# Weights in pieces of 1 MB with runs of 8192 bytes per partition, and two load buffers of 8 KB in place of three or four of 4 KB

## The chip, the cores and the metric

The kernel runs on one core of a Trainium2 chip. The metric is the device time in microseconds (us) of one execution, as the median of several runs. TensorE is PE in the profile (PEld its weight loads), VectorE is DVE, ScalarE is ACT, GpSimd is POOL, and SyncE is SP, which issues nearly all plain DMAs. In the trace, L263 means line 263 of the kernel before.

## The reference, cut to what matters

```python
def _layer(x, mem_k, mem_v, C0, n0, m0, ...):
    xn = _rmsnorm(x, g_mix)
    p = xn @ w_in + b_in                       # 1024 x 9224
    q, k, v, ig, fg, og, su, sv, xq, gates = jnp.split(p, _split_points(), axis=-1)
    ...                                        # h_a: mLSTM, h_b: spatial gating, h_c: cross-attention
    merged = g[:, :, 0] * h_a + g[:, :, 1] * h_b + g[:, :, 2] * h_c
    x = x + merged @ w_out                     # 1024 x 1024
    x = x + _peer(_rmsnorm(x, g_ffn), w_pq, k_sub1, k_sub2, u_exp, v_exp)

def _peer(xn, w_pq, k_sub1, k_sub2, u_exp, v_exp):
    q = xn @ w_pq                              # 1024 x 2048
    v1, i1 = top_k(q1 @ k_sub1.T, 16)          # 8 heads, 128 keys on each side
    v2, i2 = top_k(q2 @ k_sub2.T, 16)
    sc, pos = top_k(v1[:, None] + v2[None, :], 16)
    e, g = expert indices, softmax(sc)         # 128 of 16384 experts for each token
    a = gelu(einsum('tkd,td->tk', u_exp[e], xn))
    return einsum('tk,tkd->td', g * a, v_exp[e])
```

The layer runs for 1024 prompt tokens and 64 sample tokens with the same weights. `w_mk` and `w_mv` (1024 x 1024 each) make the memory's keys and values for the prompt. All data is float32.

## The kernel before

The tokens are nine tiles: eight of 128 rows (0 to 7) and "s" with 64. They go through the layer in three blocks, [0, 1], [2, 3, 4, s] and [5, 6, 7]. **The dense weights** are read once per block. A list `pieces` holds them in the order of use: 16 pieces for the memory, then 96 for each block (`w_in`, `w_out`, `w_pq`), then the experts. A piece is 512 KB: 128 partitions by two rows of 512 columns for `w_in` and its like (runs of 2048 bytes), by four rows of 256 columns for `u_exp_t` (runs of 1024 bytes), by two rows of 512 columns for `v_exp` (2048).

`w_load` (L253) issues one piece on SP into `wraw`, which has three buffers of 4 KB per partition; in the last stage every fourth piece goes into a fourth buffer, `wrawx`. `w_split` (L267) takes 512 columns at a time, a split, and makes two fp32r halves of it: ACT casts `wh` (L277) and DVE subtracts for `wl` (L280; 32 of them run on POOL). `wh` and `wl` have four buffers each. When the last split of a piece is done, the next `w_load` is issued. `w_get` (L287) hands a split to the matmuls: `proj_t` (L311 to L313), `proj_T` (L328 to L330), and in the last stage `hidden` (L1119 to L1121) and `dense` (L1268 to L1270), three matmuls for each product.

**The experts** are computed in two ways. For tiles 0, 1, s, 6 and 7 rows of `u_exp` and `v_exp` are gathered by POOL (L1025, 128 rows of 4096 bytes in one indirect DMA, 1152 of them) into three buffers `gu` and four `gv`, and DVE multiplies and adds them up (L1038 for u, L1046 for v). This stream (`experts`) runs beside the blocks and beside the last stage. At the 576th gather it halts until the signal "weights". For tiles 2 to 5, all 16384 experts are computed densely in the last stage: `dense` builds one-hot weights by matmul (L1210), stores them (L1221), loads them again in pieces of 1 MB with runs of 8192 bytes (L1098), and runs the two big products.

Between a block's projections and its gathers stand `retrieve` and `choose_tile`: the top 16 of every head by DVE's max, max_index and match_replace (`top16`, L797 to L803), with a work buffer `tk` (four buffers), the places `pos`, and the softmax `gg` (`ggd`). `end_u` (L954) makes a tile's gather weights, `w2` (two buffers).

Generators for these streams are merged in program order by `Flow`, with an estimated cost at each yield. Then the tile framework's scheduler sets each engine's order, and places waits where a buffer is still in use. Each engine runs its list strictly in order; SP's list holds the weight loads, the small loads and the stores together.

Of the kernel before, what the change touches and what calls it, by code (L numbers as in the profile page):

```python
# [18 lines left out]
D = 1024  # L19
# [46 lines left out]
def tile_stream_step(ctx: ExitStack, tc: tile.TileContext, a: dict, out: dict):  # L66
# [26 lines left out]
    RAW, HL = 3, 4  # L93
# [53 lines left out]
    G.dma_start(wg_raw, a["w_in"][:, O_IG:O_IG + 8].rearrange("(k p) c -> p k c", p=128))  # L147
# [96 lines left out]
    def want(src, c0):  # L244
        for kp in range(4):
            pieces.append(src[kp * 256:(kp + 1) * 256, c0:c0 + 512].rearrange("(k p) c -> p k c", p=128))
# [6 lines left out]
    def w_load():  # L253
        i = W["load"]
        if i >= len(pieces):
            return
        src = pieces[i]

        if now["dp"] is None or i % (RAW + 1):
            t = wp.tile([128, D], F32, name="wraw", bufs=RAW)  # L260
        else:
            t = now["dp"].tile([128, D], F32, name="wrawx")
        SP.dma_start(t.rearrange("p (k c) -> p k c", k=src.shape[1]), src)  # L263
        raw_t[i] = t
        W["load"] += 1

    def w_split():  # L267
        i = W["split"]
        if i >= 2 * len(pieces):
            return  # L270
        p, kk = divmod(i, 2)
        while W["load"] <= p:
            w_load()
        t = raw_t[p][:, kk * 512:(kk + 1) * 512]
        h = wp.tile([128, 512], F32R, name="wh", bufs=HL)
        l = wp.tile([128, 512], F32R, name="wl", bufs=HL)
        S.copy(h, t)  # L277

        E = G if POOL[0] <= i < POOL[1] else V
        E.tensor_tensor(l, t, h.bitcast(F32), op=ALU.subtract)  # L280
        split_t[i] = (h, l)
        W["split"] += 1
        if kk == 1:
            raw_t.pop(p)
            w_load()

    def w_get():  # L287
        i = W["got"]
        while W["split"] <= min(i + HL - 1, 2 * len(pieces) - 1):
            w_split()  # L290
        W["got"] += 1
        return split_t.pop(i)
# [276 lines left out]
    def want_block():  # L569
        for c in (O_K, O_Q, O_V, O_V + 512, O_SV, O_SV + 512, O_SU, O_SU + 512, O_GT + D, O_GT + D + 512,  # L570
                  O_XQ, O_XQ + 512, O_OG, O_OG + 512, O_GT, O_GT + 512, O_GT + 2 * D, O_GT + 2 * D + 512):
            want(a["w_in"], c)
        for c in (0, 512):
            want(a["w_out"], c)
        for c in (0, 512, 1024, 1536):
            want(a["w_pq"], c)
# [14 lines left out]
    for nm in ("w_mk", "w_mv"):  # L591
        for c in (0, 512):
            want(a[nm], c)
# [9 lines left out]
    def want_u(m):  # L603
        if m < NP:
            for r in range(2):
                pieces.append(a["u_exp_t"][r * 512:(r + 1) * 512, m * 256:(m + 1) * 256]
                              .rearrange("(k p) e -> p k e", p=128))
# [3 lines left out]
    for g in range(NP // GP):  # L611
        for j in range(2 * GP):
            if j % 2 == 0:
                want_u(GP * g + j // 2 + LG)
            hf, q = divmod(j, GP)
            e0 = (GP * g + q) * 256
            pieces.append(a["v_exp"][e0:e0 + 256, hf * 512:(hf + 1) * 512].rearrange("(k p) c -> p k c", p=128))
# [179 lines left out]
    def top16(v, i, src, n):  # L797
        w = kp.tile([128, 128], F32, name="tk", bufs=4)[0:src.shape[0]]
# [41 lines left out]
    def choose_tile(b, t):  # L840
# [67 lines left out]
        gg = kp.tile([128, 8, 16], F32, name="ggd")[0:L]  # L908
# [30 lines left out]
    def experts():  # L939
# [14 lines left out]
        def end_u(t):  # L954
# [4 lines left out]
            t1 = gp.tile([128, 128], F32, name="w2", bufs=2)[:, 0:L]  # L959
# [129 lines left out]

    w_load()  # L1090
# [213 lines left out]
def _layout(i):  # L1304
# [17 lines left out]
    d["w_in"] = c(g["w_in"][0])  # L1322
# [13 lines left out]
    d["w_mk"] = c(g["w_mk"][0])  # L1336
    d["w_mv"] = c(g["w_mv"][0])
    d["w_out"] = c(g["w_out"][0])
    d["w_pq"] = c(g["w_pq"][0])
# [3 lines left out]
    d["u_exp_t"] = c(g["u_exp"][0].T)  # L1343
# [29 lines left out]
```

## Time and profile before

| | |
|---|---|
| median of 3 runs | 3620.37 us (3608.81 to 3621.52) |
| the profiled execution | 3614.62 us, of which the span of the trace is 3612.6 us |
| busy in the span | PE 3267.4, DVE 3102.9, POOL 1669.1, ACT 1369.6 us |
| moved by DMA | 1024.77 MB, 284 GB/s; q0 (POOL's gathers) 604.58 MB, q1 (SP) 413.06 MB |

A busy share is a mean over stages that have different limits, so the profile is read by stretches: the memory and block 0 (to about 450 us), blocks 1 and 2 with the gathers beside them (to about 1770), the last retrieval and the one-hot stage (to about 2215), and the last stage with both dense products. The chain of work that ended last says which engine's work stood in a row in a stretch; the waits say how long an engine stood and what ended it.

### The profile page before, as it was taken

What the parts mean: (1) busy time and instruction counts of PE and PEld (TensorE: products, weight loads), DVE (VectorE), ACT (ScalarE), POOL (GpSimd) and SP (SyncE); (2) the same over time, 40 slices, a digit from 0 to 9 for tenths busy, and PEclk for the clock granted to TensorE, in tenths of its full rate; (3) what the DMA queues carried; (4) which work ended last, traced back from release to release, by engine and by line L of the source; (5) the groups of instructions that cost most, each with busy time, mean ns of one, the idle gap of its engine ahead of it and who ended that gap; (6) DMA issues with size and microseconds to landing.
All of it is one profiled execution on the core that took longest, in us unless ns stands there. A gap on an engine that the chain in (4) does not pass through costs nothing.

```text
span 3612.6 us, 46174 instructions
## 1 busy us (share of the span) xinstructions
PE 3267.4 (90%) x15364; PEld 2633.3 (73%) x15364; DVE 3102.9 (86%) x6493; ACT 1369.6 (38%) x2481; POOL 1669.1 (46%) x1208
## 2 busy tenths in 40 slices
PE   8999999689998488699958896999999999999998
PEld 7787876467667366576756895888778888887886
DVE  5555798868999999989998998998789888887998
ACT  5555534223333234333324673333223333332332
POOL 1000448866656672654431004565456455544654
PEclk9999999799999789799978897999999999999999
DMA  7455578889898787898876558999889999988997
GB/s 236 146 164 178 176 260 310 290 264 354 315 360 307 271 279 234 287 320 280 289 243 197 169 172 283 342 353 331 298 307 382 334 341 336 344 309 297 385 345 261
DMA packets 447436, 1024.77 MB, mean 284 GB/s; under 512 B 32183, under 2 KB 169567, under 8 KB 443101
## 3 DMA queue, kind: packets, MB, share of 16 engines
q0 software_dynamic: 166528, 604.58, 47.5%
q1 hardware_dynamic: 276828, 413.06, 34.2%
q10 hardware_dynamic: 3840, 4.20, 0.3%
q8 instruction: 120, 1.97, 0.2%
q14 instruction: 120, 0.98, 0.1%
HBM read 968.44 MB, written 53.26 MB: 283 GB/s over the span
## 4 chain that ended last, share of the span: by engine, by line
PE 66%; DVE 13%; issue 9%; DMA 7%; POOL 4%; ACT 1%; SPq 0%; DVEq 0%; POOLq 0%; ACTq 0%
PE acc L311 6%; PE acc L312 6%; PE acc L313 6%; PE ph L1121 5%; PE ph L1119 5%; PE ph L1120 5%; PE po L1270 5%; PE po L1268 5%; PE po L1269 5%; PE po L1210 4%; DMA gu<-in_u_exp_dram,e 4%; POOL gu L1025 3%; PE acc L330 3%; PE acc L328 3%; PE acc L329 3%
## 5 line engine op out<-in xcount | busy, mean ns | idle before, releaser
L277 ACT CAST wh<-wraw 128x512 fp32r<-128x512 f32 x994 | 612.8, 621 | 1352.4 <-PE ph L1120 459.7
L1025 POOL DMA_INDIRECT gv<-in_v_exp_dram,e x522 | 720.1, 1380 | 864.0 <-DVE gacc L1046 307.9
L1025 POOL DMA_INDIRECT gu<-in_u_exp_dram,e x506 | 698.6, 1381 | 606.3 <-DVE gu L1038 404.9
L280 DVE TENSOR_TENSOR wl<-wraw,wh 128x512 fp32r<-128x512 f32 x962 | 654.3, 686 | 231.5 <-ACT wh L277 228.9
L1038 DVE SCALAR_TENSOR_TENSOR gu<-gu,gx 128x1024 f32<-128x1024 f32 x506 | 613.7, 1217 | 105.5 <-DMA gu<-in_u_exp_dram,e 103.9
L1046 DVE SCALAR_TENSOR_TENSOR gacc<-gv,w,gacc 128x1024 f32<-128x1024 f32 x448 | 572.3, 1278 | 6.1 <-DMA gv<-in_v_exp_dram,e 5.7
L312 PE MATMUL acc<-wl,half 128*128 128x512 f32 (+1 forms) x1152 | 475.1, 413 | 12.0 <-DVE wl L280 10.4
L313 PE MATMUL acc<-wh,half 128*128 128x512 f32 (+1 forms) x1152 | 457.2, 403 | 0.0
L311 PE MATMUL acc<-wh,half 128*128 128x512 f32 (+1 forms) x1152 | 414.0, 411 | 18.5 <-ACT uB L470 15.7
L1268 PE MATMUL po<-wh,W 128*128 128x512 f32 x1024 | 399.4, 398 | 31.2 <-ACT W L1238 30.6
L1269 PE MATMUL po<-wl,W 128*128 128x512 f32 x1024 | 407.9, 398 | 4.5 <-DVE wl L280 4.5
L1121 PE MATMUL ph<-dxh,wl 128*128 128x512 f32 x1024 | 401.7, 392 | 7.2 <-DVE wl L280 7.1
L1270 PE MATMUL po<-wh,W 128*128 128x512 f32 x1024 | 407.2, 398 | 0.6 <-DVE W L1239 0.6
L1119 PE MATMUL ph<-dxh,wh 128*128 128x512 f32 x1024 | 400.3, 391 | 1.3 <-DVE dxl L1143 1.3
L1120 PE MATMUL ph<-dxl,wh 128*128 128x512 f32 x1024 | 399.8, 390 | 0.0
L311 PEld LDWEIGHTS acc<-wh,half 128*128 128x128 f32 (+1 forms) x1152 | 210.8, 184 | 89.3 <-ACT uB L470 16.9
L312 PEld LDWEIGHTS acc<-wl,half 128*128 128x128 f32 (+1 forms) x1152 | 212.6, 185 | 80.9 <-DVE wl L280 16.6
L328 PE MATMUL acc<-half,wh 128*128 128x256 f32 (+2 forms) x768 | 250.4, 345 | 16.9 <-ACT wh L277 13.4
L329 PE MATMUL acc<-half,wh 128*128 128x256 f32 (+2 forms) x768 | 258.6, 342 | 0.0
L313 PEld LDWEIGHTS acc<-wh,half 128*128 128x128 f32 (+1 forms) x1152 | 211.6, 185 | 54.8 <-issue 1.7
L1268 PEld LDWEIGHTS po<-wh,W 128*128 128x128 f32 x1024 | 193.8, 189 | 78.8 <-issue 32.3
L330 PE MATMUL acc<-half,wl 128*128 128x256 f32 (+2 forms) x768 | 226.8, 342 | 18.4 <-DVE wl L280 18.4
(450 smaller groups left out, 5271.1 us busy)
## 6 DMA issues: line engine op xcount, KB each, us to landing
wraw<-in_w_in_dram SPq DMA_DIRECT2D x216, 512.0 KB
wraw<-in_v_exp_dram SPq DMA_DIRECT2D x126, 512.0 KB
wraw<-in_u_exp_t_dram SPq DMA_DIRECT2D x67, 512.0 KB
gd<-sg SPq DMA_DIRECT2D x16, 2048.0 KB
g<-gd SPq DMA_DIRECT2D x32, 1024.0 KB
wrawx<-in_u_exp_t_dram SPq DMA_DIRECT2D x61, 512.0 KB
wraw<-in_w_pq_dram SPq DMA_DIRECT2D x48, 512.0 KB
wraw<-in_w_out_dram SPq DMA_DIRECT2D x24, 512.0 KB
```

The costliest lines, as they stand in the source:

```text
L277: S.copy(h, t)
L280: E.tensor_tensor(l, t, h.bitcast(F32), op=ALU.subtract)
L311: T.matmul(ps[i], xh[:, cs], h, start=(k == 0), stop=False)
L312: T.matmul(ps[i], xh[:, cs], l, start=False, stop=False)
L313: T.matmul(ps[i], xl[:, cs], h, start=False, stop=(last and b is None))
L1025: G.indirect_dma_start(out=tl, out_offset=None, in_=src, in_offset=bass.IndirectOffsetOnAxis(ap=col, axis=0))
L1038: V.scalar_tensor_tensor(tl, tl, 1.0, xn, op0=ALU.mult, op1=ALU.mult, accum_out=av[:, j:j + 1])
L1119: T.matmul(o, h[:, cs], xh[:, k + kk, :], start=(k + kk == 0), stop=False)
L1121: T.matmul(o, l[:, cs], xh[:, k + kk, :], start=False, stop=(k + kk == KD - 1))
L1268: T.matmul(o, hi, h, start=(q == 0 and k == 0), stop=False)
L1269: T.matmul(o, hi, l, start=False, stop=False)
L1270: T.matmul(o, lo, h, start=False, stop=(q == GP - 1 and k == 1))
```

## The change

The host lays the weights out again. `w_in` without the eight gate columns, `w_mk`, `w_mv`, `w_out` and `w_pq` become blocks of 128 x 2048 (four rows of 512 columns), `u_exp` blocks of 128 x 2048 (eight rows of 256 columns), `v_exp` blocks of 128 x 2048 (four rows of 512 columns). Each block is 1 MB in one stretch of memory, 8192 bytes per partition. The gate columns become an array of their own. `wraw` has two buffers of 8 KB, and `wrawx` is gone. A piece has four splits, and the next load is issued after the fourth. The first 56 pieces (the memory and block 0) are loaded by two DMAs of 4096 bytes per partition each, the others by one. An early `w_load` ahead of the last stage is gone. Beside this, `tk` goes from four buffers to two, `w2` from two to one, and `ggd` shares one buffer with `pos`.

```diff
-    RAW, HL = 3, 4
+    RAW, HL = 2, 4
+    W1 = 56
...
-    G.dma_start(wg_raw, a["w_in"][:, O_IG:O_IG + 8].rearrange("(k p) c -> p k c", p=128))
+    G.dma_start(wg_raw, a["w_gate"])
...
     def want(src, c0):
-        for kp in range(4):
-            pieces.append(src[kp * 256:(kp + 1) * 256, c0:c0 + 512].rearrange("(k p) c -> p k c", p=128))
+        for kp in range(2):
+            pieces.append(src[c0 // 512, kp])
...
-        src = pieces[i]
-
-        if now["dp"] is None or i % (RAW + 1):
-            t = wp.tile([128, D], F32, name="wraw", bufs=RAW)
-        else:
-            t = now["dp"].tile([128, D], F32, name="wrawx")
-        SP.dma_start(t.rearrange("p (k c) -> p k c", k=src.shape[1]), src)
+        t = wp.tile([128, 2 * D], F32, name="wraw", bufs=RAW)
+
+        n = D if i < W1 else 2 * D
+        for c in range(0, 2 * D, n):
+            SP.dma_start(t[:, c:c + n], pieces[i][:, c:c + n])
...
-        p, kk = divmod(i, 2)
+        p, kk = divmod(i, 4)
...
-        if kk == 1:
+        if kk == 3:
             raw_t.pop(p)
             w_load()
...
     def want_u(m):
         if m < NP:
-            for r in range(2):
-                pieces.append(a["u_exp_t"][r * 512:(r + 1) * 512, m * 256:(m + 1) * 256]
-                              .rearrange("(k p) e -> p k e", p=128))
+            pieces.append(a["u_exp_p"][m])
...
-            pieces.append(a["v_exp"][e0:e0 + 256, hf * 512:(hf + 1) * 512].rearrange("(k p) c -> p k c", p=128))
+            pieces.append(a["v_exp_p"][(GP * g + q) // 2, hf])
...
-        w = kp.tile([128, 128], F32, name="tk", bufs=4)[0:src.shape[0]]
+        w = kp.tile([128, 128], F32, name="tk", bufs=2)[0:src.shape[0]]
...
-        gg = kp.tile([128, 8, 16], F32, name="ggd")[0:L]
+        gg = kp.tile([128, 8, 16], F32, name="ggd", tag="pos", bufs=1)[0:L]
...
-            t1 = gp.tile([128, 128], F32, name="w2", bufs=2)[:, 0:L]
+            t1 = gp.tile([128, 128], F32, name="w2", bufs=1)[:, 0:L]
...
-    w_load()
```

The order of the instructions moves at three places that matter here. **SP at the start**, around the first load of the memory's values (`mv<-mvd`), which reads what ACT's queue has just stored. Before:

```order
L297 DMA bl<-bpd 3x512
L263 DMA wraw<-in_w_mv_dram 128x2x512 x8
L263 DMA wraw<-in_w_in_dram 128x2x512
L753 DMA mv<-mvd 128x2x512
L263 DMA wraw<-in_w_in_dram 128x2x512 x15
```

Of the change (a row is 512 KB here, half a piece):

```order
L296 DMA bl<-bpd 3x512
L262 DMA wraw<-in_w_mv_p_dram 128x1024 x6
L262 DMA wraw<-in_w_in_p_dram 128x1024 x2
L749 DMA mv<-mvd 128x2x512
L262 DMA wraw<-in_w_in_p_dram 128x1024 x14
```

Ahead of `mv<-mvd` now stands 1 MB of `w_in`, four splits, where 512 KB, two splits, stood.

**DVE in the last block's retrieval**, right behind the 580th split on DVE's list (the 32 splits of POOL not counted; `tk`, `i`, `v` and `sc` belong to `top16`, `gacc` is the sum over gathered v rows). Before:

```order
L803 MAX_INDEX i_15042<-v_15041,tk 128x8 x4
L800 MAX_INDEX i_15042<-v_15041,sc 128x8 x4
L1046 SCALAR_TENSOR_TENSOR gacc<-gv,w_17933,gacc 128x1024
L801 MATCH_REPLACE tk<-v_14879,sc 128x128 x4
L1046 SCALAR_TENSOR_TENSOR gacc<-gv,w_17933,gacc 128x1024
L802 MAX v_14879<-tk 128x8 x4
L799 MAX v_14879<-sc 128x8 x4
L1046 SCALAR_TENSOR_TENSOR gacc<-gv,w_17933,gacc 128x1024
```

Of the change:

```order
L279 TENSOR_TENSOR wl<-wraw,wh 128x512
L798 MAX v_14712<-tk 128x8 x2
L795 MAX v_14641<-sc 128x8 x2
L799 MAX_INDEX i_14713<-v_14712,tk 128x8
L795 MAX v_14641<-sc 128x8 x2
L799 MAX_INDEX i_14713<-v_14712,tk 128x8
L796 MAX_INDEX i_14642<-v_14641,sc 128x8 x2
L797 MATCH_REPLACE tk<-v_14712,sc 128x128
```

The gathered rows are gone from this stretch: in DVE's list the 576th gather, where the stream halts, stands ahead of split 544 now, and stood behind split 584 before. By split 400 of the list DVE has added up 33 more gathers than before, by split 544 it is 54 or 55 more. From the end of the one-hot stage on the two lists are alike again.

**SP in the last stage**. Before:

```order
L1098 DMA g_18700<-gd 128x2048
L263 DMA wrawx<-in_u_exp_t_dram 128x4x256
L263 DMA wraw<-in_u_exp_t_dram 128x4x256
L263 DMA wraw<-in_v_exp_dram 128x2x512 x2
L1098 DMA g_19180<-gd 128x2048
```

Of the change:

```order
L1092 DMA g_18440<-gd 128x2048
L262 DMA wraw<-in_u_exp_p_dram 128x2048
L262 DMA wraw<-in_v_exp_p_dram 128x2048
L1092 DMA g_18914<-gd 128x2048
L262 DMA wraw<-in_u_exp_p_dram 128x2048
```

Two loads of 1 MB stand where four of 512 KB stood; the loads of one-hot weights keep their places.

## Rows read from the trace of the kernel before

**Rows 1.** The page's sections 1 and 2: busy time of each engine, then granted clock and DMA in 40 slices of the span.

```profile
PE 3267.4 (90%) x15364; PEld 2633.3 (73%) x15364; DVE 3102.9 (86%) x6493; ACT 1369.6 (38%) x2481; POOL 1669.1 (46%) x1208
...
PEclk9999999799999789799978897999999999999999
DMA  7455578889898787898876558999889999988997
```

**Rows 2.** Busy time of each engine by stretches of the span: length, busy us (and count) of PE, PEld, DVE, ACT, POOL, then granted TensorE clock, DMA share and GB/s.

```profile
0.00:120.00 120.00, 103.97 (x555) 86.58 (x556) 63.21 (x140) 68.43 (x126) 10.56 (x23) 0.97 0.68 215
120.00:450.00 330.00, 322.61 (x1721) 265.63 (x1720) 201.29 (x569) 184.25 (x359) 41.34 (x32) 0.99 0.55 167
450.00:800.00 350.00, 304.08 (x1237) 212.45 (x1236) 299.50 (x820) 122.01 (x254) 242.27 (x144) 0.91 0.82 280
800.00:1163.00 363.00, 348.88 (x1571) 267.06 (x1570) 323.87 (x587) 129.88 (x246) 230.84 (x155) 0.99 0.91 331
1163.00:1293.00 130.00, 66.36 (x318) 58.37 (x318) 126.28 (x410) 30.34 (x53) 89.67 (x60) 0.69 0.82 278
1293.00:1530.00 237.00, 194.08 (x805) 145.54 (x804) 220.99 (x674) 92.08 (x192) 123.45 (x85) 0.88 0.80 267
1530.00:1768.00 238.00, 213.60 (x928) 168.97 (x927) 221.60 (x522) 84.04 (x163) 120.59 (x85) 0.94 0.87 292
1768.00:1980.00 212.00, 156.32 (x868) 142.37 (x867) 204.09 (x668) 80.47 (x147) 60.87 (x54) 0.83 0.74 243
1980.00:2215.00 235.00, 187.65 (x1478) 177.57 (x1477) 206.79 (x417) 148.68 (x306) 15.52 (x10) 0.86 0.62 188
2215.00:2900.00 685.00, 675.60 (x2899) 546.04 (x2899) 611.48 (x932) 211.79 (x310) 370.55 (x279) 0.99 0.93 333
2900.00:3613.00 713.00, 694.21 (x3000) 562.78 (x2998) 623.75 (x767) 217.62 (x329) 363.44 (x284) 0.99 0.91 327
```

**Rows 3.** The waits that ended with a landed weight load, from the view of the tile `wraw`: what ACT's cast L277 or DVE's L280 waited for, us in total, times.

```profile
  PE ph L1120: 459.7, 227
...
  DMA wraw<-in_w_in_dram: 48.7, 12
...
  DMA wraw<-in_w_pq_dram: 11.8, 5
```

**Rows 4.** The chain of work that ended last, from 52 to 75 us: start, length, what.

```profile
57.15 6.75 DMA mvd<-mA
63.89 0.02 SPq L753
...
64.68 5.54 DMA wraw<-in_w_in_dram
```

**Rows 5.** DMA queues from 100 to 300 us, where q1 carries weights in runs of 2048 bytes and no gather runs: packets, MB, share of 16 engines.

```profile
q1 hardware_dynamic: 15894, 30.95, 52.2%
```

**Rows 6.** The same from 2199 to 2208.2 us, where q1 carries one load of 1 MB in runs of 8192 bytes (L1098) beside gathers.

```profile
q0 software_dynamic: 490, 1.75, 54.1%
q1 hardware_dynamic: 144, 1.05, 28.1%
```

**Rows 7.** The same from 1100 to 1800 us.

```profile
q0 software_dynamic: 37302, 135.80, 57.0%
q1 hardware_dynamic: 31384, 60.87, 25.9%
```

**Rows 8.** DVE's waits for landed gathers from 450 to 1100 us: us in total, times, longest.

```profile
DVE gu L1038 <- DMA gu<-in_u_exp_dram,e: 31.8, 9, 11.7
...
DVE gv L1038 <- DMA gv<-in_u_exp_dram,e: 13.0, 7, 5.3
DVE gacc L1046 <- DMA gv<-in_v_exp_dram,e: 3.8, 5, 1.7
```

**Rows 9.** The same from 1100 to 1800 us.

```profile
DVE gu L1038 <- DMA gu<-in_u_exp_dram,e: 20.4, 15, 4.7
...
DVE gacc L1046 <- DMA gv<-in_v_exp_dram,e: 1.9, 2, 1.3
```

**Rows 10.** DVE's busy time on line L1046 alone, the sums over gathered v rows, in two stretches.

```profile
1530.00:1768.00 238.00, 69.11 (x54) 0.94 0.87 292
1768.00:1980.00 212.00, 69.14 (x54) 0.83 0.74 243
```

**Rows 11.** The chain of work that ended last from 1768 to 1980 us, by line.

```profile
by line: DVE gacc L1046 11.5%; PE acc L328 10.3%; PE acc L329 10.3%; PE acc L330 10.2%; PE po L1210 8.0%; PE ph L1119 6.6%; PE ph L1120 6.3%; PE ph L1121 6.3%; DVE tk L801 4.3%; DVE i L803 3.6%; DVE v L802 3.4%; DVE i L800 3.3%; PE ms L819 
```

**Rows 12.** Waits over the whole span around `w2` and `ggd`: us in total, times, longest.

```profile
ACT w L962 <- DVE gu L1038: 19.5, 4, 8.1
...
ACT ggd L910 <- DVE ggd L909: 18.9, 2, 15.7
```

**Rows 13.** PE's waits from 2215 us to the end.

```profile
PE ph L1121 <- DVE wl L280: 7.1, 8, 1.8
PE po L1269 <- DVE wl L280: 4.5, 5, 1.6
```

**Rows 14.** DVE's waits for landed gathers in the last stage, from 2215 to 2900 us.

```profile
DVE gu L1038 <- DMA gu<-in_u_exp_dram,e: 38.4, 36, 3.3
```

**Rows 15.** The page's section 6: indirect DMAs of u rows, count, median us from issue to landing.

```profile
gu<-in_u_exp_dram,e POOLq DMA_INDIRECT x506, 6.6
```

More of the change, by code (lines that the diff above doesn't have):

```diff
@@ L268, in w_split @@
         i = W["split"]
-        if i >= 2 * len(pieces):
+        if i >= 4 * len(pieces):
             return
-        p, kk = divmod(i, 2)
+        p, kk = divmod(i, 4)
         while W["load"] <= p:
@@ L288, in w_get @@
         i = W["got"]
-        while W["split"] <= min(i + HL - 1, 2 * len(pieces) - 1):
+        while W["split"] <= min(i + HL - 1, 4 * len(pieces) - 1):
             w_split()
@@ L571, in want_block @@
                   O_XQ, O_XQ + 512, O_OG, O_OG + 512, O_GT, O_GT + 512, O_GT + 2 * D, O_GT + 2 * D + 512):
-            want(a["w_in"], c)
+            want(a["w_in_p"], c - (8 if c > O_FG else 0))
         for c in (0, 512):
-            want(a["w_out"], c)
+            want(a["w_out_p"], c)
         for c in (0, 512, 1024, 1536):
-            want(a["w_pq"], c)
+            want(a["w_pq_p"], c)
     def main():
@@ L592, in tile_stream_step @@
         for c in (0, 512):
-            want(a[nm], c)
+            want(a[nm + "_p"], c)
     for _ in BLOCKS:
@@ L611, in tile_stream_step @@
     for g in range(NP // GP):
-        for j in range(2 * GP):
-            if j % 2 == 0:
-                want_u(GP * g + j // 2 + LG)
+        for j in range(0, 2 * GP, 2):
+            want_u(GP * g + j // 2 + LG)
             hf, q = divmod(j, GP)
-            e0 = (GP * g + q) * 256
-            pieces.append(a["v_exp"][e0:e0 + 256, hf * 512:(hf + 1) * 512].rearrange("(k p) c -> p k c", p=128))
+            pieces.append(a["v_exp_p"][(GP * g + q) // 2, hf])
     def mlstm():
@@ L1321, in _layout, with parts @@
     d["g_mem_t"] = c(g["g_mem"][0].reshape(8, 128).T)
-    d["w_in"] = c(g["w_in"][0])
+    w = g["w_in"][0]
+    d["w_gate"] = c(w[:, O_IG:O_IG + 8].reshape(8, 128, 8).transpose(1, 0, 2))
+    def parts(m):
+        return c(m.reshape(2, 4, 128, -1, 512).transpose(3, 0, 2, 1, 4).reshape(-1, 2, 128, 2048))
+    d["w_in_p"] = parts(np.concatenate([w[:, 0:O_IG], w[:, O_OG:]], axis=1))
     d["b_in"] = c(b)
@@ L1335, in _layout @@
     d["b_s_t"] = c(bs)
[L1336 to L1339, printed above, removed]
+    d["w_mk_p"] = parts(g["w_mk"][0])
+    d["w_mv_p"] = parts(g["w_mv"][0])
+    d["w_out_p"] = parts(g["w_out"][0])
+    d["w_pq_p"] = parts(g["w_pq"][0])
     d["k_sub_t"] = c(np.stack([g["k_sub1"][0].T, g["k_sub2"][0].T], axis=1))
@@ L1342, in _layout @@
     d["v_exp"] = c(g["v_exp"][0])
-    d["u_exp_t"] = c(g["u_exp"][0].T)
+    d["u_exp_p"] = c(g["u_exp"][0].reshape(64, 256, 8, 128).transpose(0, 3, 2, 1).reshape(64, 128, 2048))
+    d["v_exp_p"] = c(g["v_exp"][0].reshape(32, 2, 2, 128, 2, 512).transpose(0, 4, 3, 1, 2, 5).reshape(32, 2, 128, 2048))
     return d
```

## The prediction

> **What bounds the kernel now.** I read the busy times first, then the same times by stretches, then the chain in those stretches, and the DMA views last. Over the span PE is busy for 90% and DVE for 86% [rows 1], which says little, since the stretches differ [rows 2]. To 450 us PE is busy for 426.6 of 450 us at a clock of 0.97 to 0.99 while DMA stands at 0.55 to 0.68: PE is the bound, and loads have room. From 450 to 1768 us DVE leads: 126.3 of 130 us from 1163 to 1293, where PE has 66.4, and 442.6 of 475 us from there to 1768. PE waits for DVE's retrieval there, and its clock falls to 0.69 and 0.88. From 1768 to 2215 us DVE (410.9 of 447) and PE (343.9) are near each other. From 2215 us on PE is the bound: 1369.8 of 1398 us, at a clock of 0.99, although DMA is at 0.91 to 0.93.
>
> So where are the weight loads waited for at all? The splits waited 48.7 us for pieces of `w_in` and 11.8 us for pieces of `w_pq`, 60.5 us in 17 waits, against 459.7 us for one line of matmuls alone [rows 3]. No piece of `u_exp` or `v_exp` stands in that list. The load that this change makes more efficient is late on few occasions, and never in the long last stage. That limits what it can give.
>
> **The change part by part.**
>
> *The start.* SP holds the weight loads and `mv<-mvd` in one list, and stands for 6.75 us until the stored values have landed; the next weight load then takes 5.54 us more [rows 4]. Before, 512 KB of `w_in`, two splits, had been issued ahead of it; now it is 1 MB, four splits. Two splits more are two casts and two steps of work for PE. Block 0 has 96 pieces, 192 splits, and lies mostly in the 330 us from 120 to 450 [rows 2], 1.7 us each, so two cover some 3.5 us of the 5.54, and the time to their landing a little more. I take -4 us; the bounds are 0 (the larger piece lands later) and -6.
>
> *The packets.* From 100 to 300 us, with runs of 2048 bytes and no gathers, q1 used 52.2% of 200 us for 30.95 MB: 104.4 / 30.95 = 3.37 us of all 16 engines per MB [rows 5]. One load with runs of 8192 bytes used 28.1% of 9.2 us for 1.05 MB: 2.46 us per MB [rows 6]. That is 0.91 us per MB less. From 1100 to 1800 us, mixed with gathers, q1 cost 25.9% of 700 us for 60.87 MB, 2.98 us per MB [rows 7], which would leave 0.52. Blocks 1 and 2 load 192 pieces of 524 KB, 100.7 MB, so 52 to 92 us of DMA time go out of 1318 us, 4 to 7%. Who feels it? DVE, which waited 31.8 + 13.0 + 3.8 us for gathers to 1100 us and 20.4 + 1.9 us after, 70.9 us [rows 8, 9]. If these waits fall with the load on the engines, it is 3 to 5 us. If half of them go, since a queue shortens faster than its load, it is 35. POOL's issue and the seven gather buffers end part of these waits too, and those stay. I take -5; bounds 0 and -35. In the last stage u rows go from 1024 to 8192 bytes and save more DMA time, but there no PE time hangs on it: of PE's waits only 7.1 + 4.5 us go back to a split [rows 13]. I take 0.
>
> The Trainium skill weighs this differently. "DMA: Bandwidth & Descriptors", section "Anatomy of one DMA", gives a DMA some 2.0 us of fixed cost beside its bytes over 436 GB/s; 224 DMAs fewer (560 to 336) would by that be an estimated 448 us, if each stood on the path. The 60.5 us of waits above show that they don't, and the trace decides.
>
> *The smaller lead.* A load is issued four splits ahead of its need, as before where three buffers stand, and four instead of six where there were four; now it brings 1 MB. In the last stage four splits take 4 x 1398 / 520 = 10.8 us (some 520 splits there), and 1 MB by itself takes 2.5 us [rows 6]; with gathers beside it perhaps three times that. `wh` and `wl` hold four more splits. I take 0, and name the cover: if a load took over 10 us, ACT's cast would be late, and over 20 us PE.
>
> *The order.* This is the largest term, and the title doesn't show it. DVE now has its 576th gather ahead of split 544; before, 54 sums over v rows lay from 1768 to 1980 us, 69.1 us of DVE's time [rows 10]. They move ahead, into 1163 to 1768 us. DVE is idle there for 605 - 568.9 = 36.1 us [rows 2]. If all of it is filled, the stretch grows by 33 us, if none, by 69. What does the stretch from 1768 us give back? DVE loses 69.1 of its 204.1 us, but PE needs 156.3 of the 212, so at most 55.7 us. The chain there has 11.5% on L1046, 24.4 us [rows 11], which is what surely goes. The net lies between 33 - 55.7 = -23 and 69 - 24.4 = +45 us. I take +10, near the middle: rows 2 show DVE saturated on one side, and PE with much idle time on the other.
>
> *The buffers.* `tk` is written and read by DVE alone, which runs in order: 0. `ggd` in `pos`'s place puts the softmax behind the cast of `pos`; nine tiles, of which ACT waited 18.9 us in two [rows 12], with DVE busy elsewhere: 0 to 5. `w2` with one buffer lets `end_u` begin only behind the last v row of the tile before, one sum of 1.28 us later, four times; ACT stood 19.5 us at these four places already [rows 12]. Together +1, bounds 0 and +10, covered by u gathers that go on meanwhile. The gate columns and the fewer issues on SP: 0, neither is waited for.
>
> *The sum*: -4 - 5 + 0 + 10 + 1 = +2 us on the profiled execution's 3614.6, 3616.6 us, so **3617**. That execution lies 5.8 us below the median of 3620.4 and inside the runs' spread of 12.7 us.
>
> **The rivals.**
>
> *Gathers flow faster.* For it: DMA stands at 0.80 to 0.91 from 450 to 1768 us, and landed gathers are what DVE waited for most [rows 2, 8, 9]. Against: 70.9 us is all there is. With half of it (-35), the start at -6 and the order at -5: 3569 us.
>
> *Every wait for weights goes.* The splits' 60.5 us [rows 3] are the most that a cheaper load can give directly: 3554 us. The skill's fixed cost per DMA, cited above, is the rule behind it. Against: the one that I followed came from an SP list that stood before the load was issued [rows 4], which a cheaper load does not cure.
>
> *The order costs its full price.* The early stretch is DVE's, and takes 69 us; the late one gives back 24, since PE's own chain of products and retrieval stays: +45, with -4 and -5 some 3651 us. It decides from the point where 1163 to 1768 us grows by more than 1768 to 2215 shrinks.
>
> *Gathers slow down in the last stage.* q1's 8192-byte packet takes 41.4 / 128 = 0.32 us of an engine, a 2048-byte one 104.4 x 16 / 15894 = 0.105 [rows 5, 6]. A gather of 128 rows puts 8 packets on each engine; if each waits for one weight packet, that is 8 x 0.22 = 1.7 us more beside a median of 6.6 us to landing [rows 15]. DVE has 1398 - 1235.2 = 163 us of slack for 576 gathers, 0.28 us each; beyond this DVE sets the pace, and each 0.1 us costs 58. Loads run for some 40% of the time, so 0.35 us may be reached: 0.07 x 576 = +40, 3657 us. Against: the same bytes pass in fewer bursts, so the mean delay of a gather stays, and DVE waited 38.4 us in 36 waits, no more [rows 14]. The skill's "DMA: Bandwidth & Descriptors", section "Queues, rings and completion order", says that an engine takes turns between queues packet by packet, which would make this share rise; no row here shows the turns themselves.
>
> *The runs don't pay.* If q1's time per MB stays near 2.98 us, the packets' term is 0: 3622 us, within the forecast's case.
>
> **How the numbers follow.** Forecast (little change): 0.43, 3602 to 3638. Gathers faster: 0.28. All waits for weights gone: 0.05. The order at its full price: 0.15. The last stage slower: 0.09. A measurement of this kernel can tell about 0.5%, 18 us, from no change, so faster means under 3602 us. Faster 0.33, same 0.43, slower 0.24. The range reaches into the rivals on both sides and leaves out the ends of each: 3560 to 3655. Cases of both signs hold 0.57; the forecast's own range is 3602 to 3638.
>
> **What would show it.** Right: q1's time per MB from 1100 to 1800 us falls to 2.5 us or less; 1163 to 1768 us is longer and 1768 to 2215 shorter, by 20 us or more each; the last stage begins within 20 us of 2215 us and keeps its 1398 us; the weight load behind `mv<-mvd` leaves the chain. Wrong: DVE's waits for gathers fall below 40 us to 1800 us (the first rival), PE waits for splits over 30 us in the last stage or DVE's waits for gathers there double (the fourth), or the one-hot stage begins over 30 us later (the third).

## The result: slower, 1.0114 of the time before

The changed kernel took 3661.0 us, the median of four runs (3647.5 to 3671.0), against 3618.5 us for the kernel before beside it: a ratio of 1.0114 with an interval of 1.0082 to 1.0146. Six more runs later gave 3652.6 us and 1.0104 (1.0077 to 1.0131), so I speak of about 40 us. The forecast was 3617, its range ended at 3655.

The profiled execution took 3671.0 us, its span is 3669.2 us. First the page of the changed kernel: busy times, then granted clock and DMA in 40 slices.

```profile
PE 3268.7 (89%) x15364; PEld 2631.8 (72%) x15364; DVE 3104.6 (85%) x6493; ACT 1369.6 (37%) x2481; POOL 1656.4 (45%) x1208
...
PEclk9999998799999669699898998999999999999999
DMA  7455478789898877899762558989879999988997
```

PE and DVE do the same work as in [rows 1], to 1 or 2 us. So the 57 us of span that were added are idle time. The clock shows a first place: slices 14 and 15, 1192 to 1376 us, stand at 0.6 where [rows 1] have 0.7 and 0.8.

The next view cuts the changed kernel by its own progress: at splits 400, 544 and 592 on DVE, and 27 us ahead of split 608, as [rows 2] are cut for the kernel before at 1293, 1768, 1980 and 2215 us (columns as there).

```profile
1163.00:1350.00 187.00, 67.81 (x347) 59.37 (x346) 167.82 (x477) 34.16 (x59) 126.45 (x89) 0.66 0.82 279
1350.00:1856.00 506.00, 412.33 (x1733) 314.27 (x1732) 466.57 (x1161) 178.77 (x355) 258.73 (x191) 0.89 0.84 286
1856.00:2035.00 179.00, 159.17 (x956) 146.77 (x955) 166.01 (x692) 86.67 (x164) 3.62 (x3) 0.91 0.42 144
2035.00:2256.00 221.00, 178.82 (x1398) 169.43 (x1397) 188.52 (x366) 140.20 (x288) 13.01 (x9) 0.88 0.61 188
2256.00:2941.00 685.00, 666.53 (x2833) 538.55 (x2832) 593.07 (x913) 206.57 (x303) 371.83 (x271) 0.98 0.88 323
```

The first stretch has 187 us where [rows 2] have 130, with as much PE work (67.8 and 66.4 us) and 41 us more of DVE's. The first two together last 693 us where the kernel before takes 605. DVE is busy for 634.4 us of them instead of 568.9, and idle for 58.6 instead of 36.1. The third has 179 us in place of 212: there the early gathers give something back. In the last stage DMA is busy for 0.88 in place of 0.93.

What DVE does more of is in its groups by line from 1163 to 1400 us (count, busy us, mean ns), of the kernel before and then of the change: 53 sums over v rows where there were 38, as many products with u rows, and 38 splits where there were 57.

```profile
L1046 DVE SCALAR_TENSOR_TENSOR gacc<-gv,w,gacc 128x1024 f32<-128x1024 f32 x38 | 48.2, 1269 | 0.1
L1038 DVE SCALAR_TENSOR_TENSOR gu<-gu,gx 128x1024 f32<-128x1024 f32 x53 | 63.8, 1207 | 8.2 <-DMA gu<-in_u_exp_dram,e 8.2
L280 DVE TENSOR_TENSOR wl<-wraw,wh 128x512 fp32r<-128x512 f32 x57 | 37.3, 673 | 1.5 <-ACT wh L277 1.5
```

```profile
L1042 DVE SCALAR_TENSOR_TENSOR gacc<-gv,w,gacc 128x1024 f32<-128x1024 f32 x53 | 67.5, 1274 | 3.3 <-DMA gacc<-x2d 2.7 <-DMA gv<-in_v_exp_dram,e 0.6
L1034 DVE SCALAR_TENSOR_TENSOR gu<-gu,gx 128x1024 f32<-128x1024 f32 x54 | 65.4, 1212 | 19.0 <-DMA gu<-in_u_exp_dram,e 18.9
L279 DVE TENSOR_TENSOR wl<-wraw,wh 128x512 fp32r<-128x512 f32 x38 | 25.4, 676 | 0.0
```

Who pays is in the waits from 1100 to 2260 us: PE's products for the scores of the retrieval wait for ACT, which copies the scores to `sc`, and ACT waits for a buffer of `sc` that DVE has not searched yet. First PE's and ACT's wait in the kernel before, then the two in the change:

```profile
PE ms L819 <- ACT sc L822: 61.0, 8, 13.0
ACT sc L822 <- DVE tk L801: 93.3, 12, 13.3
```

```profile
PE ms L815 <- ACT sc L818: 86.7, 6, 24.4
ACT sc L818 <- DVE tk L797: 104.9, 12, 21.5
```

The table counts DVE's subtractions `wl` and gathered sums (products with u rows and sums over v rows together) in the traces: when split k came, how long it was from split 608, some 27 us into the last stage, to the last of DVE's splits ("last stage"), and how many gathered sums its list has ahead of splits 400 and 544. Times are of the one profiled execution (its own time in the column before the last), the median is that of all runs.

```
kernel               tk  sums ahead   split   split   split   last    this   median
                         400   544     400     544     608    stage   exec.
before                4  350   521   1293.2  1767.9  2242.1  1344.4  3614.6  3618.5
change                2  383   576   1350.8  1856.3  2282.7  1357.4  3671.0  3661.0
change again (e9)     2  383   576   1338.3  1838.6  2263.2  1353.1  3647.1  3652.6
before, tk 2 (e1)     2  384   568   1329.4  1812.4  2250.8  1354.0  3632.9  3638.0
change, tk 4 (e3)     4  350   531   1294.0  1781.7  2248.7  1355.9  3636.9  3636.7
change, tk 5 (e18)    5  339   518   1274.5  1748.6  2224.8  1352.8  3609.7  3617.4
before, tk 5 (e16)    5  343   522   1276.4  1750.7  2224.8  1346.8  3599.3  3597.4
before, tk 6 (e17)    6  328   520   1268.0  1784.2  2252.3  1352.1  3632.7  3624.6
before, no tk (e8)    -  335   521   1295.0  1791.8  2265.1  1343.3  3636.3  3627.6
change, no tk (e4)    -  329   516   1276.6  1760.5  2240.3  1351.1  3619.6  3637.9
layout only (e2)      4  350   521   1296.2  1774.3  2247.9  1358.6  3634.6  3627.3
all but 1 MB (e13)    2  384   576   1340.3  1847.2  2269.8  1354.9  3652.6  3651.5
```

From split 384 to 544 the change is longer by 84 us (689.0 against 604.9; 77 in the second profile), from 544 to 608 shorter by 48 (50).

The weight loads: what the splits waited for (compare [rows 3]), and q1 from 1100 to 1800 us ([rows 7]) and from 100 to 300 us ([rows 5]).

```profile
  DMA wraw<-in_w_in_p_dram: 30.6, 11
  DMA wraw<-in_u_exp_p_dram: 25.4, 10
```

```profile
q1 hardware_dynamic: 10461, 54.10, 21.0%
```

```profile
q1 hardware_dynamic: 9049, 30.73, 47.2%
```

A MB costs 0.210 x 700 / 54.10 = 2.72 us in place of 2.98, and 3.07 in place of 3.37. Pieces of `w_in` are waited for 18 us less in this profile; in the second one of the change it is 45.8 us, 3 us less, so this gain is not sure. Pieces of `u_exp` are now waited for, 25.4 and 31.0 us, where the kernel before waited 1.9 us for `wraw` and 1.4 for `wrawx`. DVE's waits for gathers in the blocks, from 450 to 1100 and then from 1100 to 1800 us, did not fall against [rows 8, 9]:

```profile
DVE gu L1034 <- DMA gu<-in_u_exp_dram,e: 29.8, 17, 5.5
...
DVE gv L1034 <- DMA gv<-in_u_exp_dram,e: 16.6, 6, 4.6
...
DVE gacc L1042 <- DMA gv<-in_v_exp_dram,e: 6.4, 3, 3.3
```

```profile
DVE gu L1034 <- DMA gu<-in_u_exp_dram,e: 26.4, 23, 2.8
...
DVE gacc L1042 <- DMA gv<-in_v_exp_dram,e: 3.1, 2, 2.5
```

They add up to 82.3 us, and to 67.4 in the second profile, where those rows have 70.9. In the last stage, from 2215 to 2900 us, DVE waits longer for gathers than in [rows 14], and from 2215 us to the end PE waits 18.7 us for splits where [rows 13] have 11.6:

```profile
DVE gu L1034 <- DMA gu<-in_u_exp_dram,e: 66.6, 38, 5.8
```

```profile
PE ph L1115 <- DVE wl L279: 12.9, 8, 3.3
PE po L1263 <- DVE wl L279: 5.8, 3, 3.2
```

### The profile page after: what moved, and what is told of

The parts are those of the page before. It is cut to its first block, busy times and chain, and to the rows that moved or that the text cites. A ratio compares the mean times of both kernels' runs of the same rounds, so it can differ in the third digit from the quotient of the medians.

```text
span 3669.2 us, 45561 instructions
## 1 busy us (share of the span) xinstructions
PE 3268.7 (89%) x15364; PEld 2631.8 (72%) x15364; DVE 3104.6 (85%) x6493; ACT 1369.6 (37%) x2481; POOL 1656.4 (45%) x1208
## 4 chain that ended last, share of the span: by engine, by line
PE 45%; issue 8%; DVE 7%; DMA 4%; POOL 4%; ACT 1%; POOLq 0%; DVEq 0%; SPq 0%; ACTq 0%
PE po L1264 5%; PE po L1263 5%; PE po L1262 5%; PE ph L1115 5%; PE ph L1113 5%; PE ph L1114 5%; PE po L1204 5%; POOL gu L1021 3%; DMA gu<-in_u_exp_dram,e 2%; PE acc L311 2%; PE acc L310 2%; PE acc L312 2%; DVE gacc L1042 1%; DVE gu L1034 1%; PE acc L327 1%
## 5 line engine op out<-in xcount | busy, mean ns | idle before, releaser
L276 ACT CAST wh<-wraw 128x512 fp32r<-128x512 f32 x1120 | 689.4, 621 | 1484.4 <-PE ph L1114 471.3
L1021 POOL DMA_INDIRECT gv<-in_v_exp_dram,e x522 | 739.9, 1417 | 887.6 <-DVE gacc L1042 306.9
L1021 POOL DMA_INDIRECT gu<-in_u_exp_dram,e x506 | 674.1, 1332 | 592.8 <-DVE gu L1034 385.2
L279 DVE TENSOR_TENSOR wl<-wraw,wh 128x512 fp32r<-128x512 f32 x1088 | 737.7, 684 | 235.6 <-ACT wh L276 232.1
L312 PE MATMUL acc<-wh,half 128*128 128x512 f32 (+1 forms) x1152 | 458.8, 404 | 0.0
L310 PE MATMUL acc<-wh,half 128*128 128x512 f32 (+1 forms) x1152 | 422.3, 414 | 16.9 <-ACT uB L469 15.3
L1115 PEld LDWEIGHTS ph<-dxh,wl 128*128 128x128 f32 x1024 | 193.4, 189 | 57.4 <-DVE wl L279 16.7
```

The lines of the kernel that those rows point to most:

```text
L310: T.matmul(ps[i], xh[:, cs], h, start=(k == 0), stop=False)
L312: T.matmul(ps[i], xl[:, cs], h, start=False, stop=(last and b is None))
L1021: G.indirect_dma_start(out=tl, out_offset=None, in_=src, in_offset=bass.IndirectOffsetOnAxis(ap=col, axis=0))
L1115: T.matmul(o, l[:, cs], xh[:, k + kk, :], start=False, stop=(k + kk == KD - 1))
```

## The experiments

My theory after reading the traces: `tk`'s two buffers make the scheduler put the gathers ahead on DVE, and the delay of the retrieval is most of the loss. The rival: the 1 MB pieces and their layout cost it. In the ratios below the kernel before is 1.

**`tk` alone.**

```diff
-        w = kp.tile([128, 128], F32, name="tk", bufs=4)[0:src.shape[0]]
+        w = kp.tile([128, 128], F32, name="tk", bufs=2)[0:src.shape[0]]
```

> The kernel before with one edit: the work buffer `tk` of the top-16 search has two buffers in place of four. Pieces, layout and load buffers stay those of before. In DVE's list this alone puts 384 gathered sums ahead of split 400 (before 350, the change 383) and 568 ahead of split 544 (before 521, the change 576). Theory (the two `tk` buffers move the gathers ahead, and that is most of the loss): 3645 to 3660 us, split 400 on DVE at 1340 to 1355 us (before 1293), split 544 some 80 us later than before, the last stage begins 30 to 45 us later. Rival (the 1 MB pieces and their lead cost the time, the order does not): within 10 us of before, 3610 to 3628 us.

Measured: 3638.0 us, 1.0062 (1.0045 to 1.0078). Split 400 came at 1329 us and split 544 44 us late; 9 us were left at split 608. The profiled run's span is 18 us longer, and the other 9 or 10 us came in the last stage, which took 1354.0 us with the weights and load buffers of the kernel before. Its order had moved too: at the same split there DVE is between 4 sums behind the kernel before and 2 ahead (the change: between 6 behind and 2 ahead), so the two lists are alike from the one-hot stage on only in the large. The direction and the place are the theory's, the size is half of what I expected. PE's waits show the same mark as the change:

```profile
PE ms L819 <- ACT sc L822: 97.9, 8, 24.9
```

**The change with `tk` mended**, by four buffers and without any.

```diff
-        w = kp.tile([128, 128], F32, name="tk", bufs=2)[0:src.shape[0]]
+        w = kp.tile([128, 128], F32, name="tk", bufs=4)[0:src.shape[0]]
...
-            av = gp.tile([128, 128], F32, name="av", bufs=2)
+            av = gp.tile([128, 128], F32, name="av", bufs=1)
```

> The changed kernel with `tk` at four buffers again; the room comes from `av` (one buffer in place of two) and `rs` (three in place of four). 1 MB pieces, two load buffers, `ggd` and `w2` stay as in the change. DVE's list has 350 gathered sums ahead of split 400 again (change 383) and 531 ahead of split 544 (change 576, before 521). Theory (order by `tk`): 3615 to 3635 us: the 40 us at the start of the last stage come back, the 13 to 15 us that the last stage itself lost stay. Rival (1 MB pieces): 3650 to 3665 us, as the change.

```diff
-        w = kp.tile([128, 128], F32, name="tk", bufs=2)[0:src.shape[0]]
+        w = src
```

> The changed kernel without `tk` at all: the match_replace of the top-16 search writes over its own source, which is not read afterwards. Everything else is the change. DVE's list has 329 gathered sums ahead of split 400 (change 383, before 350) and 516 ahead of split 544 (576, 521). Theory (order by `tk`: the fewer gathers ahead of the retrieval, the earlier the retrieval ends): 3605 to 3632 us, split 400 at or before before's 1293 us. Rival (1 MB pieces): 3650 to 3665 us. A third possibility: with the gathers pushed later than before, the last stage has more of them to carry, and the time ends near 3640 us.

Measured: 3636.7 us, 1.0053 (1.0038 to 1.0067), and 3637.9 us, 1.0052 (1.0036 to 1.0068). Split 400 is back at 1294 us with four buffers, and from 1163 to 1400 us DVE's sums over v rows fall from 53 to 36:

```profile
L1042 DVE SCALAR_TENSOR_TENSOR gacc<-gv,w,gacc 128x1024 f32<-128x1024 f32 x36 | 45.8, 1273 | 0.0
```

Some 19 us of the ten runs' median of 3655.5 come back, with the 1 MB pieces still in place; 18 us stay. Both lie above what the theory expected, the second near the third possibility.

**The layout alone**: everywhere, in the blocks, in the last stage, and in the last stage without longer runs. The pieces stay 512 KB, DVE's order is that of before.

```diff
-            pieces.append(src[kp * 256:(kp + 1) * 256, c0:c0 + 512].rearrange("(k p) c -> p k c", p=128))
+            pieces.append(src[c0 // 512, kp])
...
-                pieces.append(a["u_exp_t"][r * 512:(r + 1) * 512, m * 256:(m + 1) * 256]
-                              .rearrange("(k p) e -> p k e", p=128))
+                pieces.append(a["u_exp_p"][m, r])
```

> The kernel before with the host's layout alone: pieces of 512 KB as before, each in one stretch of memory with runs of 4096 bytes per partition, three or four load buffers and four `tk` buffers as before; DVE's order is that of before. Theory (`tk`'s order is the loss, the layout by itself is harmless): 3600 to 3620 us, q1 at 2.5 to 2.7 us of all engines per MB from 1100 to 1800 us (before 2.98). Rival (weights in long runs hold up the gathers and so cost the time): over 3630 us, with DVE's waits for gathers over the span well above before's 104 us.

> The kernel before with the contiguous layout (runs of 4096 bytes, pieces of 512 KB) for the memory and the three blocks alone; the expert weights of the last stage stay in runs of 1024 and 2048 bytes. DVE's order is that of before. With the layout everywhere the median was 8.8 us above before. Theory A (long runs hold the gathers up in the last stage): 3614 to 3621 us, no loss. Theory B (the loss lies in the blocks): 3624 to 3630 us.

> The kernel before with the contiguous layout (runs of 4096 bytes, pieces of 512 KB) for the expert weights of the last stage alone. Theory A (long runs hold the gathers up in the last stage): 3624 to 3630 us, and DVE's waits for gathers from 2250 to 2850 us above before's 36.7 us, near the 53.5 us of the layout everywhere. Theory B (the loss lies in the blocks): 3614 to 3621 us.

```diff
-                pieces.append(a["u_exp_p"][m, r])
+                pieces.append(a["u_exp_p"][m, r].rearrange("k p e -> p k e"))
```

> The kernel before with the last stage's weights stored so that each 512 KB piece is one stretch of memory, but read in runs of the old length (u 1024 bytes, v 2048). With runs of 4096 bytes in the same stretches the median was 3623.2, 5 us above before. If the run's length is what slows the last stage: 3616 to 3621 us. If it is where the bytes lie: 3621 to 3626 us.

Measured: everywhere 3627.3 us, 1.0027 (1.0018 to 1.0036); blocks 3619.4 us, 1.0002 (0.9993 to 1.0011); last stage 3623.2 us, 1.0013 (1.0004 to 1.0022); stretches without long runs 3617.8 us, 0.9998 (0.9987 to 1.0010). I had expected the layout to be harmless, and it is not: it costs 9 us, and gains nothing where it was to gain. The half that can be placed lies in the last stage. Gathers are waited for longer there from 2250 to 2850 us, with the layout everywhere

```profile
DVE gu L1037 <- DMA gu<-in_u_exp_dram,e: 53.5, 33, 3.6
```

where the kernel before has 36.7 us in that stretch and the change 66.6. That the run's length does it and not the place of the bytes is what the last of the four says, but its interval and that of the third overlap. The traces point the same way. Six kernels have the same gathered sums ahead of each split of the last stage: with the old runs it took 1344.4, 1349.4 and 1348.3 us (before, blocks, stretches without long runs), with runs of 4096 bytes 1358.6, 1351.5 and 1355.5 (everywhere, last stage, and the change in 512 KB with four `tk` buffers below), 8 us more on the mean. In these last three no split of that stage waited for a weight load, so the load itself was not late; with the layout everywhere PE waited 20.8 us for DVE's splits there (11.6 before), behind DVE's longer waits for gathers.

**The size of a packet in the 1 MB pieces**: 4096 bytes to the end; the change again beside 4096 bytes in the blocks alone and 2048 bytes; and 4096 bytes with four `tk` buffers.

```diff
-    W1 = 56
+    W1 = 1000
```

> The changed kernel with each piece of 1 MB loaded by two DMAs of 4096-byte runs to the end, not only in its first 56 pieces. The same bytes come in the same bursts, in packets of half the size. If the length of a packet is what costs the last stage its 13 us: 3650 us or less, DVE's waits for gathers from 2250 to 2850 us at 50 to 55 us (change 66.6). If the burst of 1 MB is what costs it: 3655 to 3668 us, waits near 66 us.

> The changed kernel once more, so that its median and a second profile stand on the same chip and in the same call as the next three. Both theories: 3655 to 3665 us. In the second profile split 400 at 1340 to 1352 us, split 608 some 30 to 40 us behind before's 2242, DVE's waits for gathers from 2250 to 2850 us at 60 to 70 us.

```diff
-    W1 = 56
+    W1 = 152
```

> The changed kernel with two DMAs of 4096-byte runs for all pieces of the memory and the three blocks, and one DMA of 8192-byte runs only in the last stage. If 8192-byte packets hold the gathers up in blocks 1 and 2: as with halves to the end, 3644 to 3650 us, split 544 some 15 to 20 us earlier than the change's. If they do so in the last stage: 3655 to 3663 us.

```diff
-        n = D if i < W1 else 2 * D
+        n = D if i < W1 else D // 2
```

> The changed kernel with runs of 2048 bytes behind its first 56 pieces: each piece of 1 MB is loaded by four DMAs of 256 KB, issued together. If the packet's length is what costs (8192 bytes 3661 us, 4096 bytes 3647): 3635 to 3648 us, waits for gathers from 2250 to 2850 us at 60 us or less. If more DMAs help by being more, or the step from 8192 to 4096 was chance: 3645 to 3662 us. DVE's list has 568 gathered sums ahead of split 544 (576), so up to 5 us may come from that.

> The changed kernel with both mends together: four `tk` buffers (room from `av` and `rs`) and two DMAs of 4096-byte runs for every piece of 1 MB. DVE's list has 350 gathered sums ahead of split 400 and 530 ahead of split 544 (before 350, 521). If the order by `tk` (some 24 us) and the 8192-byte packets (some 14 us) are two causes that add up: 3617 to 3627 us. If the halves only helped because they changed how the early gathers fell in the changed kernel's order: 3632 to 3640 us, as with `tk` alone mended (3636.7).

Measured: 3646.9, 3652.6, 3656.1, 3656.7 and 3634.9 us. The first looked like a gain of 14 us over 3661; but the change itself came out at 3652.6 us, quarters gained nothing, and halves with four `tk` buffers are where those buffers are without halves (3636.7). The waits for gathers from 2250 to 2850 us stayed above the kernel before's in all of them. So the packet inside a 1 MB piece makes no difference that I can measure, and the first reading was the scatter of the change's runs (3646 to 3674 us).

**The 1 MB pieces taken out**: the whole change, and the change with four `tk` buffers, both in pieces of 512 KB with runs of 4096 bytes, three or four load buffers and the early `w_load`.

```diff
-    RAW, HL = 2, 4
+    RAW, HL = 3, 4
...
-        for kp in range(2):
+        for kp in range(4):
             pieces.append(src[c0 // 512, kp])
```

> The change without its 1 MB pieces: contiguous layout in pieces of 512 KB with runs of 4096 bytes, three or four load buffers of 4 KB as before, and all the small edits (`tk` two, `w2` one, `ggd` in `pos`'s place). DVE's order is the change's at the places spoken of: 384 gathered sums ahead of split 400, 576 ahead of split 544. If the 1 MB pieces and the two buffers cost nothing: 3650 to 3660 us, as the change. If they own the open rest: 3640 to 3648 us (`tk` alone 3638, with the layout's 5 to 9 on top).

> The change with four `tk` buffers (room from `av` and `rs`), as two runs before (3636.7 and 3634.9 us), but in pieces of 512 KB with runs of 4096 bytes and three or four load buffers. DVE's order is that of those two runs: 353 gathered sums ahead of split 400 (350), 530 ahead of split 544 (531 and 530). If the open rest belongs to the small edits and the gathers that they move: 3633 to 3640 us. If it belongs to the 1 MB pieces: 3625 to 3630 us, as the layout alone (3627.3).

Measured: 3651.5 us, 1.0085 (1.0072 to 1.0097), and 3641.6 us, 1.0053 (1.0036 to 1.0070). The second equals its twin with 1 MB pieces (1.0053), the first lies 4 us under the change's ten runs, with intervals that overlap. As the main cause the rival falls: by the medians piece and buffers of 1 MB cost 0 to some 5 us, though the intervals leave room for more. Beside `tk` and the layout, the mended kernel's rest goes with 9 or 10 gathered sums more ahead of split 544 (530 against 521). The small edits (`w2`, `ggd`) are in both kernels and were never run alone; that they bring these sums, and that the sums cost the rest, is not shown.

**More `tk` buffers**: none, five and six in the kernel before (the last with one `w2` buffer in place of two), and five in the change.

```diff
-        w = kp.tile([128, 128], F32, name="tk", bufs=4)[0:src.shape[0]]
+        w = kp.tile([128, 128], F32, name="tk", bufs=5)[0:src.shape[0]]
```

> The kernel before without `tk`: the match_replace of the top-16 search writes over its source. DVE's list has 335 gathered sums ahead of split 400 (before 350) and 521 ahead of split 544 (521). Theory (order by `tk`; four buffers are nearly enough): 3608 to 3622 us, split 400 some 15 us earlier than before's 1293 us, and little of it left at the start of the last stage, as in the changed kernel without `tk`. Rival (the place of the gathers costs nothing, the two-buffer loss came from waits on the buffer itself): split 400 at 1293 us, 3618 us.

> The kernel before with five `tk` buffers in place of four. DVE's list has 343 gathered sums ahead of split 400 (before 350, with two buffers 384, without `tk` 335) and 522 ahead of split 544 (521). If the time follows the gathers ahead of split 400: 3610 to 3617 us. If four buffers lie at a bottom, as the run without `tk` (3627.6) says: 3617 to 3626 us.

> The kernel before with six `tk` buffers and one `w2` buffer in place of two. DVE's list has 328 gathered sums ahead of split 400 (five buffers 343, four 350, two 384, without `tk` 335), 520 ahead of split 544 (522, 521, 568, 521). If fewer gathers ahead of the last retrieval always pay: 3580 to 3597 us, split 400 before 1276 us. If the gathers that are pushed back have to be carried later: 3600 to 3630 us, like the run without `tk` (3627.6), with split 400 early and split 464 or 608 late again.

```diff
-        w = kp.tile([128, 128], F32, name="tk", bufs=2)[0:src.shape[0]]
+        w = kp.tile([128, 128], F32, name="tk", bufs=5)[0:src.shape[0]]
...
-            go = gp.tile([128, 128], F32, name="gg", bufs=3)
+            go = gp.tile([128, 128], F32, name="gg", bufs=2)
```

> The changed kernel with five `tk` buffers; the room comes from `av` (one), `rs` (three) and `gg` (two in place of three). 1 MB pieces, two load buffers, `w2` one, `ggd` in `pos`'s place. DVE's list has 339 gathered sums ahead of split 400 and 518 ahead of split 544 (five buffers in the kernel before: 343, 522). If the order is all but the last stage's 8 us: 3603 to 3612 us. If the 1 MB pieces or the smaller edits cost the 16 us that stood with four buffers: 3612 to 3622 us. If `gg`'s missing buffer holds the gathers back: over 3630 us.

Measured: none 3627.6 us, 1.0025 (1.0014 to 1.0036); five 3597.4 us, 0.9944 (0.9926 to 0.9963); six 3624.6 us, 1.0010 (1.0001 to 1.0019); the change with five 3617.4 us, 0.9992 (0.9982 to 1.0002). Five buffers in the kernel before beat both kernels, by 23 and by 58 us. That is below both ranges that I had written down, and the run without `tk` is above its two. With five, split 400 came 17 us earlier than before's, and all 17 were still there at split 608; but 11.5 of them stood at split 384 already (1151.5 us, before 1163.0), ahead of the last retrieval, and `tk` at two buffers was as early there (1151.1). So the last retrieval itself gave some 5 of the 17. The change with five lies 17 to 20 us above the kernel before with five (by the ratios and by the medians), so its other parts cost about that much there. PE's wait for the scores, 61.0 us in the kernel before and 86.7 in the change, is shorter with five:

```profile
PE ms L819 <- ACT sc L822: 42.2, 6, 14.3
```

But the dose does not go on. With six, split 400 came earlier still, at 1268 us, and split 544 late, at 1784. The stretch between these two splits, in the run with five and then in the run with six buffers (windows as above):

```profile
1276.00:1751.00 475.00, 400.65 (x1729) 307.79 (x1728) 450.07 (x1200) 176.65 (x354) 261.85 (x175) 0.92 0.85 286
```

```profile
1268.00:1784.00 516.00, 409.82 (x1725) 312.25 (x1724) 475.30 (x1240) 176.22 (x357) 275.25 (x190) 0.89 0.84 280
```

DVE has 25 us more to do there, since gathers not taken ahead of split 400 come between (193 sums against 176, 1.27 us each), and stands idle for 41 us instead of 25. So fewer gathers ahead of split 400 do not always pay, and this count alone does not foretell the time. What share the `w2` buffer has in the run with six was not tested.

## Why the prediction was wrong, by its own steps

*The start* (-4): right. Split 191, near the end of block 0, came at 352.0 and 350.1 us in the two profiles of the change, 352.9 before; in all nine profiles with 1 MB pieces it came at 349.7 to 352.0, in the eleven others at 352.1 to 355.9, some 3 us later on the mean. In one of the change's two profiles nothing is left of this at split 256 (698.7 and 692.5, before 696.1).

*The packets* (-5): 0. A MB became 0.26 us cheaper from 1100 to 1800 us, half of the 0.52 that I had taken, and nothing felt it: DVE's waits for gathers to 1800 us were 82.3 and 67.4 us in place of 70.9, and the change took 3656.1 us with runs of 4096 bytes in the blocks and 3652.6 with 8192, with intervals that overlap. The rival *Gathers flow faster* falls with it; *The runs don't pay* describes this term. *Every wait for weights goes* did not come either: 30.6 and 45.8 us of waits for `w_in` stayed, and waits for `u_exp` came. The Trainium skill, "DMA: Bandwidth & Descriptors", section "Bandwidth", advises to batch DMAs to 1 MiB or more. In time per MB the trace agrees in direction (2.72 us against 2.98); in the kernel's time 512 KB and 1 MB gave the same 1.0053, as one would expect of loads issued ahead of their need. The Trainium skill's fixed cost per DMA (the same page, "Anatomy of one DMA"), from which the prediction works out 448 us, is given there for DMAs that GpSimd issues. The loads here are issued by SP, and 224 DMAs fewer saved nothing.

*The order* (+10): the step that failed in size, and it carries the result. The early stretch grew by 84 us (77 in the second profile), not by 33 to 69, and the late one gave back 48 (50): +36 and +28. Two things were mis-sized. I let DVE's 36.1 us of idle time absorb part of the gathers. It absorbed none and grew to 58.6: DVE's waits for landed gathers are 30.7 us in this stretch in place of 16.2, and PE waits for the search. And I chose the middle of bounds from -23 to +45, although the row for the early side was a sum of known work (69.1 us, [rows 10]). *The order costs its full price* was the rival that came true, by its own point of decision (and its sign: the one-hot stage, split 592, began 57 us later, 39 in the second profile), and its 3651 us is the nearest number. That it is so near is in part luck: it has +45 for the order, where the traces have +36 and +28 and `tk` alone cost 20, and nothing for the last stage.

*The buffers* (+1): "`tk` is written and read by DVE alone, which runs in order: 0" was wrong. DVE does not wait for `tk` (the view of this tile in the change lists 216 searches through it and no idle time ahead of them), but the buffer count is an input of the scheduler, and two buffers alone set the order: 384 sums ahead of split 400 in the kernel before with nothing else changed, and 20 us. I read the order correctly from the listing, and put it down to the change as a whole. Why the scheduler decides so was not opened. The waits around `ggd` and `w2`, which I had priced, fell (14.0 and 12.3 us in place of 18.9 and 19.5 in [rows 12]); what these two edits do to the order was not run.

*The smaller lead* (0) and *the last stage* (0): the stage from split 608 on takes 1357.4 and 1353.1 us instead of 1344.4. One pair of profiles can't size this, since `tk` alone gave 1354.0; the six kernels with one and the same order there say some 8 us for runs of 4096 bytes. That "no PE time hangs on it" failed: PE's waits for splits rose from 11.6 to 18.7 us. I had read from [rows 3] that no piece of `u_exp` is waited for, but that list shows only its longest entries (1.9 us lay below its end). In the change ACT waits 25.4 us for `u_exp`, the lead's part; yet with the layout alone the stage was as long with no wait for a weight load. The rival *Gathers slow down in the last stage* is true in kind, its +40 was some 5 to 10. The waits for gathers rose by 28 us from 2215 to 2900 us, not to the double. That an engine takes turns between queues packet by packet (the Trainium skill, "DMA: Bandwidth & Descriptors", section "Queues, rings and completion order") does not settle it: the page's packet is a group of some 9 to 17 descriptors, not one run as in the profile's count, and no run here shows the turns. The layout runs point at the run's length, but 2048-byte runs in 1 MB pieces did not cure it (their last stage took 1358.8 us), so the mechanism stays open.

In all, of the ten runs' 37 us: two `tk` buffers some 20, the layout 9, each shown by an edit of its own, and some 8 that remain for the small edits and perhaps the 1 MB pieces, and that these runs don't divide further. The effects are not quite additive: in pieces of 512 KB four `tk` buffers gave back 10 us, in pieces of 1 MB 19.

## What to carry to other kernels

Where a scheduler sets the order, the number of buffers of a small scratch tile is a scheduling choice: change one count at a time, and compare the order on the busiest engine for each edit by itself. Here gathers put ahead of a search that another engine waits for cost their full busy time and more there (84 us for 65 us of work), and gave back 48 us later. Loads that were issued ahead of their need gained nothing from longer runs, and DVE waited longer for the gathers beside them.

## What the runs showed of the hardware that I had not expected

Runs of 4096 bytes in place of 2048 saved little in the mixed stretch from 1100 to 1800 us, where q1 with the layout alone reads

```profile
q1 hardware_dynamic: 19007, 60.55, 25.4%
```

which is 2.94 us per MB against 2.98 [rows 7]. Over all profiles the same sum gives 2.95 to 3.09 us with runs of 2048 bytes, 2.85 to 2.94 with 4096 and 2.71 to 2.82 with 8192. In the last stage a smaller DMA share (0.88 in place of 0.93) went with longer waits for gathers (66.6 in place of 38.4 us), so the busy share of the DMA engines did not tell how long DVE waits for one.
